# MLP and second norm of a streaming encoder step: four engines in program order, weight splits one tile ahead

## Chip, cores and metric

One core of a Trainium2 chip. The time is that of one execution of the program on the device, in microseconds (us), the median of several runs.

## What is computed

One layer of a hybrid streaming encoder for 512 prompt and 64 sample tokens (576 in all), width 1024, in float32 inputs and outputs: a modulated norm, a joint input projection, sparse attention beside a convolution module, an output projection, and then the part that the change concerns:

```python
x = x + g1 * (mix @ w_out)
h = rms_norm(x, norm2_g) * (1 + sc2) + sh2
x = x + g2 * (jnp.square(jax.nn.relu(h @ w_ff1)) @ w_ff2)
...
y_prompt = rms_norm(yp, final_g)
y_sample = rms_norm(ys, final_g)
```

`w_ff1` is 1024 x 4096, `w_ff2` 4096 x 1024. Prompt and sample have their own modulation (sc2, sh2, g2).

## The kernel before

Activations lie transposed, features on partitions, tokens along the free axis. The 576 tokens are taken in two halves of 288 (`JS`), and for the last MLP part as 320 and 256 (`LS`).

**Three matmuls for one.** Each weight tile (1024 x 128, eight blocks of 128 rows) is split into a rounded high part and the rest, both fp32r. ScalarE writes the high part (`whi`), GpSimd subtracts to get the low part (`wlo`). Activations are split likewise. `mm3` (lines 286 to 290) then multiplies high by high, high by low and low by high into one PSUM bank. So one weight tile and one token half take 24 matmuls, and a tile 48. `whi` and `wlo` have two buffers each, the raw tiles three.

**Before the MLP.** Up to the first half of the output projection, weight tiles come through `fetch`, `split` and `take` (lines 309 to 330): `take` starts the load of the tile two ahead, hands out a split tile, and issues the split of the next one in two halves of 512 columns.

**Second norm.** `out_half(mixT, norm2)` (lines 1081 to 1098) is the second half of the output projection, 192 matmuls in 16 groups on three rotating banks `ps_acc`. Behind each group `residual` (line 1078, VectorE) adds into `x`. Behind each feature tile `norm2` (lines 1182 to 1196) squares the tile on ScalarE, adds the squares into `s2x` on VectorE, and makes `h`, the operand of the first layer: ScalarE the high part, VectorE the low part. The row scale (`rbc`) is made from `s2x` later, by `spread` (lines 987 to 1004), while the first matmuls of the MLP run.

**MLP.** The 4096 hidden features are taken in four parts of eight tiles. For each part the first layer (`ff1`, lines 1218 to 1249) makes eight activation tiles `a`, and the second layer (`ff2`, `ff2_front`, lines 1251 to 1265) multiplies them with eight tiles of `w_ff2` into `x`. Where the second layer follows the first (called a join here), `ff2_front` runs the blocks of the first seven activation tiles for the first weight tiles, and then those of the eighth. To evacuate a half of `ff1`, VectorE multiplies by the row scale into `z`, ScalarE applies Relu with the bias, VectorE squares, ScalarE writes the high part of `a`, VectorE the low part (lines 1242 to 1248).

**What sets the order.** Through the output projection and the MLP the order of TensorE is the program's only within `out_half`. Everything else in the MLP, on all engines, is ordered by the scheduler. Weight tiles are loaded and split by `load_w` and `split_w` (lines 156 to 168), in whole tiles. The first tile of each part and layer, and all eight of the last second layer, get buffers of their own, named `wl`:

```python
def own_w():
    return [ft_([128, NK, 128], FR, "wl") for _ in range(2)]
...
hi, lo, _ = split_w("f1", *(own_w() if m == 0 else ()))
```

**The end.** The last part runs all eight tiles on the first 320 tokens, then transposes and finishes three row tiles (`final`, `finish`, lines 1293 to 1314), then runs the other 256 tokens with the last two row tiles between and behind.

## Time and profile before

| what | value |
|---|---|
| median of 3 runs | 887.25 us (885.54 to 888.99) |
| profiled execution | 887.81 us, of which 885.8 us span (first to last instruction) |
| mean granted TensorE clock | 0.963 |
| busy, share of the span | TensorE 92%, VectorE 58%, ScalarE 45%, GpSimd 33% |

The profile is of one execution. Engines: PE is TensorE's matmuls, PEld its weight loads, DVE VectorE, ACT ScalarE, POOL GpSimd, SP the engine that issues the loads. A name as L113 is a line of the kernel; a helper's line stands for all that call it, so L104 is every copy of ScalarE. Times in the trace count from the start of the span. [...] A row of idle time names what the engine waited for last.

### The profile page before, as it was taken

Reading aid. Unit: us, or ns where it says so; the run is one execution under the profiler, and the core shown is the slowest. Engines: PE = TensorE matmul, PEld = TensorE weight load, DVE = VectorE, ACT = ScalarE, POOL = GpSimd, SP = SyncE. Lnnn points to the kernel's source line nnn. Section 1 sums busy time; section 2 is a strip of 40 time slices with the busy share of each in tenths; the row PEclk is TensorE's granted clock in tenths of the full one; section 3 lists DMA queues with packets and bytes.
Section 4 is the critical chain, followed back from the end, with each engine's and each line's share of the span. In section 5 each row is a group of like instructions: output and inputs, shape, how many; then the busy total and the mean of one; then the engine's idle time right before and its main releaser. Section 6 shows DMA issues by size and latency. Waiting matters only on the chain. (4 is left out here: it accounts for less than half of the span.)

```text
span 885.8 us, 17048 instructions
## 1 busy us (share of the span) xinstructions
PE 815.4 (92%) x6787; PEld 758.7 (86%) x6787; DVE 509.6 (58%) x1133; ACT 402.0 (45%) x897; POOL 294.9 (33%) x273
## 2 busy tenths in 40 slices
PE   4898997977988999999899899998999989999996
PEld 3697894657877888989899899997999989999995
DVE  3579879999996344645856412663126631266343
ACT  5365554555876787554454211442124421244322
POOL 1155423122435323232423243332433333333700
PEclk9799998989999999999999899998999989999999
DMA  8984165445434356542312223222232223222411
GB/s 233 302 219 122 36 179 131 118 97 145 114 94 120 100 153 177 161 120 72 90 41 85 72 72 90 79 72 72 72 96 73 72 72 87 81 72 72 143 61 47
DMA packets 164553, 95.55 MB, mean 108 GB/s; under 512 B 7699, under 2 KB 161119, under 8 KB 164475
## 3 DMA queue, kind: packets, MB, share of 16 engines
q1 hardware_dynamic: 164475, 94.48, 38.3%
q8 instruction: 53, 0.87, 0.4%
q14 instruction: 25, 0.20, 0.1%
HBM read 88.82 MB, written 5.64 MB: 107 GB/s over the span
## 5 line engine op out<-in xcount | busy, mean ns | idle before, releaser
L113 POOL TENSOR_TENSOR wlo<-wraw,whi 128x1024 fp32r<-128x1024 f32 x52 | 125.0, 2403 | 239.0 <-ACT whi L104 230.0
L288 PE MATMUL ps_acc<-h,whi 128*128 128x288 f32 (+1 forms) x608 | 190.2, 313 | 0.0
L289 PE MATMUL ps_acc<-h,whi 128*128 128x288 f32 (+1 forms) x608 | 181.2, 298 | 0.0
L290 PE MATMUL ps_acc<-h,wlo 128*128 128x288 f32 (+1 forms) x608 | 180.8, 297 | 0.0
L104 ACT ACTIVATE whi<-wraw 128x512 fp32r<-128x512 f32 (+1 forms) x112 | 90.6, 823 | 151.4 <-PE ps_acc L289 49.0
L323 POOL TENSOR_TENSOR wlo<-wraw,whi 128x512 fp32r<-128x512 f32 x60 | 80.0, 1349 | 159.3 <-ACT whi L104 159.0
L288 PEld LDWEIGHTS ps_acc<-h,whi 128*128 128x128 f32 x608 | 115.9, 191 | 14.0 <-issue 12.7
L289 PEld LDWEIGHTS ps_acc<-h,whi 128*128 128x128 f32 x608 | 116.1, 191 | 0.9
L290 PEld LDWEIGHTS ps_acc<-h,wlo 128*128 128x128 f32 x608 | 116.0, 191 | 0.0
L1246 DVE TENSOR_TENSOR z<-z 128x288 f32<-128x288 f32 x64 | 79.3, 1242 | 43.4 <-ACT z L1245 43.4
L1078 DVE SCALAR_TENSOR_TENSOR x<-ps_acc,mod,x 128x288 f32<-128x288 f32 (+4 forms) x90 | 35.8, 422 | 95.5 <-PE ps_acc L290 95.3
L104 ACT ACTIVATE a<-z 128x288 fp32r<-128x288 f32 x64 | 28.2, 443 | 79.4 <-DVE z L1246 79.4
L555 DVE SCALAR_TENSOR_TENSOR yc<-u,cw,yc 128x606 f32<-128x606 f32 x60 | 58.6, 984 | 0.6
L1245 ACT ACTIVATE z<-z,bs 128x64 f32<-128x64 f32 (+2 forms) x96 | 39.9, 449 | 34.4 <-DVE z L1242 34.3
L113 DVE TENSOR_TENSOR a<-z,a 128x288 fp32r<-128x288 f32 x64 | 35.4, 556 | 29.7 <-ACT a L104 28.7
L738 ACT ACTIVATE gc<-sful,sg 128x544 bf16<-128x544 f32 x48 | 35.8, 746 | 32.1 <-DVE sg L736 31.3
L288 PE MATMUL ps_acc<-a,whi 128*128 128x288 f32 x168 | 49.9, 297 | 0.0
L290 PE MATMUL ps_acc<-a,wlo 128*128 128x288 f32 x168 | 49.9, 297 | 0.0
L289 PE MATMUL ps_acc<-a,whi 128*128 128x288 f32 x168 | 49.8, 297 | 0.0
L289 PE MATMUL ps_lg<-h,whi 128*128 128x290 f32 (+1 forms) x160 | 47.4, 296 | 0.0
L290 PE MATMUL ps_lg<-h,wlo 128*128 128x290 f32 (+1 forms) x160 | 47.3, 296 | 0.0
L288 PE MATMUL ps_lg<-h,whi 128*128 128x290 f32 (+1 forms) x160 | 47.2, 295 | 0.0
(359 smaller groups left out, 2110.1 us busy)
## 6 DMA issues: line engine op xcount, KB each, us to landing
wraw<-w_ff SPq DMA_DIRECT2D x64, 512.0 KB
ada<-w_ada SPq DMA_DIRECT2D x44, 512.0 KB
wraw<-w_in SPq DMA_DIRECT2D x24, 512.0 KB
wraw<-w_out SPq DMA_DIRECT2D x8, 512.0 KB
rep<-ud SPq DMA_DIRECT2D x24, 115.0 KB
xtok<-x_prompt SPq DMA_DIRECT2D x4, 512.0 KB
ada<-w_ada SPq DMA_DIRECT2D x8, 256.0 KB
ct<-cache_k SPq DMA_DIRECT2D x8, 256.0 KB
```

What stands on the lines that cost most here:

```text
L104: act.activation(out, in_, AF.Copy, scale=1.0 if scale is None else scale)
L113: eng.tensor_tensor(out, a, b, op=OP.subtract)
L288: pe.matmul(out, lhsT=hi, rhs=src[:, 0, cs_], start=first, stop=False)
L289: pe.matmul(out, lhsT=hi, rhs=src[:, 1, cs_], start=False, stop=False)
L290: pe.matmul(out, lhsT=lo, rhs=src[:, 0, cs_], start=False, stop=last)
L323: behind[0] = pool.tensor_tensor(lo[:, c], raw[:, c], f(hi[:, c]), op=OP.subtract).ins
L555: dve.scalar_tensor_tensor(yc[c], src, w, yc[c], op0=OP.mult, op1=OP.add)
L738: act.activation(eq, sful, AF.Sign, bias=cands[:, z:z + 1], scale=-1.0, accum_out=cnts[:, z:z + 1])
L1078: dve.scalar_tensor_tensor(xm[:, a:b], t[:, a - r.start:b - r.start], mod[:, g, s, m:m + 1], xm[:, a:b], op0=OP.mult, op1=OP.add)
L1245: act.activation(q, q, AF.Relu, bias=bs[:, s:s + 1])
L1246: dve.tensor_tensor(z[:, 1, r], z[:, 0, r], z[:, 0, r], op=OP.mult)
```

## The change

Four edits, all between the second half of the output projection and the end. First, TensorE, ScalarE, VectorE and GpSimd follow the program's order there (`manual_schedule`); before, only TensorE did, and in `out_half` alone. Second, the MLP's weight tiles join the one line of `fetch`, `split` and `take`, so each is split in two halves while the tile before it is multiplied; only the last eight get buffers of their own (`stay`). The front-first order at a join now covers one tile (two at the last join) instead of two (four). Third, in the evacuation ScalarE squares, into the PSUM bank that the matmuls have left, and VectorE copies and subtracts from there; these two are put off (`owed`, `settle`) until behind VectorE's next product. Fourth, `norm2` runs by token halves, its squares go to PSUM, and its VectorE work is put off likewise. At the end, the three first row tiles are finished between the last groups, and the last two together.

```diff
+    for part in range(NP_):
+        order += [f_rows(w_ff1, 0, 128 * (KP * part + m)) for m in range(KP)]
+        order += [f_rows(w_ff2, 128 * KP * part, 128 * m) for m in range(NK)]
+    stay = []
...
-            hi = wgt.tile([128, 1024], FR, name="whi", tag="whi", bufs=2)
-            lo = wgt.tile([128, 1024], FR, name="wlo", tag="wlo", bufs=2)
+            hi, lo = stay.pop(0)() if len(stay) > len(raws) + len(order) else [
+                wgt.tile([128, 1024], FR, name=nm, tag=nm, bufs=2) for nm in ("whi", "wlo")]
...
-                done(m)
+                    done(m, j)
...
+    mlp = ExitStack()
+    mlp.enter_context(tc.manual_schedule(engines={mybir.EngineType.PE, mybir.EngineType.Activation, mybir.EngineType.DVE,
+                                                  mybir.EngineType.Pool}))
     act.activation(ssq[:, 7:8], eps, AF.Sqrt)
...
-            act.activation(s2[:, 1], xm, AF.Square)
-            dve.tensor_tensor(s2[:, 0], s2[:, 0], s2[:, 1], op=OP.add)
...
+    s2 = ft_([128, TOK], FT, "s2x")
+    h2 = [ft_([128, 2, TOK + 2], FR, "h2") for _ in range(NK)]
+    for m, h in enumerate(h2):
         copy_to(act, h[:, 0, TOK:], mod[:, SH2, :, m])
+    for m, h in enumerate(h2):
         sub(dve, h[:, 1, TOK:], mod[:, SH2, :, m], f(h[:, 0, TOK:]))
...
-    with tc.manual_schedule(engines={mybir.EngineType.PE}):
-        out_half(mixT, norm2)
+    owed = []
+    def settle():
+        while owed:
+            owed.pop(0)()
+    def norm2(m, j):
+        xm, h, r = x1[m // 2][:, m % 2], h2[m], JS[j]
+        settle()
+        q = p_tp()[:, :HALF]
+        segs = [(slice(HALF * j + o, HALF * j + e), mod[:, SC2, s, m:m + 1]) for o, e, s in SEGS[j]]
+        for c, a in segs:
+            act.activation(h[:, 0, c], xm[:, c], AF.Copy, scale=a)
+        act.activation(q, xm[:, r], AF.Square)
+        def rest():
+            for c, a in segs:
+                dve.scalar_tensor_tensor(h[:, 1, c], xm[:, c], a, f(h[:, 0, c]), op0=OP.mult, op1=OP.subtract)
+            if m == 0:
+                copy_to(dve, s2[:, r], q)
+            else:
+                dve.tensor_tensor(s2[:, r], q, s2[:, r], op=OP.add)
+        owed.append(rest)
+    out_half(mixT, norm2)
+    settle()
...
+    def weight():
+        return [w.rearrange("p (k c) -> p k c", k=NK) for w in take()]
+    def group(t, w, src, r, ks):
+        for k in ks:
+            mm3(t, (w[0][:, k], w[1][:, k]), src[k], r, k == 0, k == NK - 1)
+    FRONT, LAST = range(NK - 1), range(NK - 1, NK)
+    JX = (slice(0, HALF), slice(HALF, TOK + 2))
+    def ff1(ts, parts=(range(NK),)):
+        w = weight()
+        for ks in parts:
             for j in (1, 0):
...
+                if j not in ts:
+                    ts[j] = p_ff()[:, :HALF + 2 * j]
+                group(ts[j], w, h2, JX[j], ks)
             yield
...
+    def ff1_evac(ts):
         a = ft_([128, 2, TOK], FR, "a")
-        z = big.tile([128, 2, TOK], FT, name="z", tag="b")
+        z = mt([128, TOK], FT, "z")
         bs = sml.tile([128, 2], FT, name="bs", tag="bs")
         copy_to(dve, bs, ts[1][:, HALF:HALF + 2])
...
-            dve.tensor_tensor(z[:, 0, r], ts[j][:, :HALF], rbc[:, r], op=OP.mult)
+        def half(j):
+            r, q = JS[j], ts[j][:, :HALF]
+            dve.tensor_tensor(z[:, r], q, rbc[:, r], op=OP.mult)
+            settle()
             for o, e, s in SEGS[j]:
-                q = z[:, 0, HALF * j + o:HALF * j + e]
-                act.activation(q, q, AF.Relu, bias=bs[:, s:s + 1])
-            dve.tensor_tensor(z[:, 1, r], z[:, 0, r], z[:, 0, r], op=OP.mult)
-            copy_to(act, a[:, 0, r], z[:, 1, r])
-            sub(dve, a[:, 1, r], z[:, 1, r], f(a[:, 0, r]))
...
+                y = z[:, HALF * j + o:HALF * j + e]
+                act.activation(y, y, AF.Relu, bias=bs[:, s:s + 1])
+            act.activation(q, z[:, r], AF.Square)
+            def rest():
+                copy_to(dve, a[:, 0, r], q)
+                sub(dve, a[:, 1, r], q, f(a[:, 0, r]))
+            owed.append(rest)
+        half(1)
+        half(0)
+        return a
+    def first_layer(part):
+        a_ = []
+        if part == 0:
+            t0, t1 = {}, {}
+            g = ff1(t0, (FRONT, LAST))
+            scales = spread(s2, 1.0 / D, rbc, dg)
+            next(g)
+            pump(scales, 1)
+            pump(g, 2)
+            pump(ff1(t1), 2)
+            pump(scales, 2)
+            a_ += [ff1_evac(t0), ff1_evac(t1)]
+        while len(a_) < KP:
+            t = {}
+            pump(ff1(t), 2)
+            a_.append(ff1_evac(t))
+        settle()
+        return a_
+    def second_layer(ws, ms, a_, rs):
+        gs = [(m, r, p_ff()[:, :r.stop - r.start]) for m in ms for r in rs]
+        for m, r, t in gs:
+            group(t, ws[m], a_, r, FRONT)
+        for m, r, t in gs:
+            group(t, ws[m], a_, r, LAST)
             residual(t, r, m, G2)
...
     for part in range(NP_ - 1):
...
+        a_ = first_layer(part)
+        for m in range(NK):
+            ws = {m: weight()}
+            if m == 0:
+                second_layer(ws, (m,), a_, JS[::-1])
+            else:
+                for r in JS:
+                    t = p_ff()[:, :HALF]
+                    group(t, ws[m], a_, r, range(NK))
+                    residual(t, r, m, G2)
+    def kept(m):
+        if m < 4:
+            return [big.tile([128, 1024], FR, name="wl", tag="b") for _ in range(2)]
+        return [ft_([128, 1024], FR, "wl") for _ in range(2)]
+    stay += [lambda m=m: kept(m) for m in range(NK)]
+    a_ = first_layer(NP_ - 1)
...
+    def finish(i0, i1, ys):
+        n = LT[i0][1]
+        v = fs[:n, i0:i1]
+        dve.tensor_reduce(v[:, :, 4:5], v[:, :, :4], axis=AX.X, op=OP.add)
+        act.activation(v[:, :, 5:6], v[:, :, 4:5], AF.Sqrt, bias=eps[:n], scale=1.0 / D)
+        dve.reciprocal(v[:, :, 6:7], v[:, :, 5:6])
...
+    ws = [weight(), weight()]
+    second_layer(ws, (0, 1), a_, LS[:1])
+    for m in range(2, NK):
+        ws.append(weight())
+        t = p_ff()[:, :320]
+        group(t, ws[m], a_, LS[0], range(NK))
+        residual(t, LS[0], m, G2)
     ys = [big.tile([128, D], FT, name="y", tag="b") for _ in range(2)]
     for m in range(NK):
...
+        t = p_ff()[:, :TOK - 320]
+        group(t, ws[m], a_, LS[1], range(NK))
+        residual(t, LS[1], m, G2)
+        if m < 3:
+            o, n = LT[m]
+            y = ft_([128, D], FT, "y")
+            final(m, o, n, (0, 1, 2, 3), y, p_lg)
+            final(m, o, n, (4, 5, 6, 7), y, p_tp)
+            finish(m, m + 1, (y,))
         for ks in ((0, 1, 2, 3), (4, 5, 6), (7,)):
             if ks[-1] == m:
                 for i, p in ((3, p_lg), (4, p_tp)):
                     final(i, *LT[i], ks, ys[i - 3], p)
...
+    finish(3, 5, ys)
```

The order rows below name tiles as the trace does: `whi`, `wlo`, `wl` are weight parts, `wraw` a raw tile, `z` and `a` as above, `h_...` the first layer's operand, `ps_...` PSUM banks; a trailing number such as 128x288 is the size, x2 a repetition.

ScalarE at the first join, where the last tiles of the first layer (part 0) are evacuated. Before:

```order
L104 ACTIVATE whi<-wraw 128x1024
L1245 ACTIVATE z<-z,bs 128x288
L104 ACTIVATE a<-z 128x288
L1245 ACTIVATE z<-z,bs 128x224
L1245 ACTIVATE z<-z,bs 128x64
L104 ACTIVATE a<-z 128x288
L104 ACTIVATE wl<-wraw 128x1024
L104 ACTIVATE whi<-wraw 128x1024
L1245 ACTIVATE z<-z,bs 128x288
L104 ACTIVATE a<-z 128x288
L104 ACTIVATE whi<-wraw 128x1024 x7
```

The first second-layer tile (`wl`) and the second (`whi`) were split between the two halves of the last evacuation. Now, the last two evacuations and what stands between and behind them:

```order
L1266 ACTIVATE z<-z,bs 128x224
L1266 ACTIVATE z<-z,bs 128x64
L1267 ACTIVATE ps_lg<-z 128x288
L1266 ACTIVATE z<-z,bs 128x288
L1267 ACTIVATE ps_lg<-z 128x288
L106 ACTIVATE whi<-wraw 128x512 x2
L1266 ACTIVATE z<-z,bs 128x224
L1266 ACTIVATE z<-z,bs 128x64
L1267 ACTIVATE ps_acc<-z 128x288
L1266 ACTIVATE z<-z,bs 128x288
L1267 ACTIVATE ps_acc<-z 128x288
L106 ACTIVATE whi<-wraw 128x512 x18
```

An evacuation is the five rows from `L1266 ... 128x224` to its second Square. The split of the join's first tile is the row `whi x2` between the last two evacuations; the second tile's is the first two of the eighteen halves behind the last one.

ScalarE behind the second norm, from the row scale to the split of the fourth tile (tile 3). Before:

```order
L104 ACTIVATE rbc<-ps_tp 128x512
L104 ACTIVATE rbc<-ps_tp 128x64
L1245 ACTIVATE z<-z,bs 128x288
L1245 ACTIVATE z<-z,bs 128x224
L1245 ACTIVATE z<-z,bs 128x64
L1245 ACTIVATE z<-z,bs 128x224
L104 ACTIVATE a<-z 128x288
L1245 ACTIVATE z<-z,bs 128x64
L1245 ACTIVATE z<-z,bs 128x288
L104 ACTIVATE a<-z 128x288 x3
L104 ACTIVATE whi<-wraw 128x1024
```

The scheduler mixed the first two tiles' evacuations. Now:

```order
L106 ACTIVATE rbc<-ps_tp 128x64
L1266 ACTIVATE z<-z,bs 128x224
L1266 ACTIVATE z<-z,bs 128x64
L1267 ACTIVATE ps_lg<-z 128x288
L1266 ACTIVATE z<-z,bs 128x288
L1267 ACTIVATE ps_lg<-z 128x288
L1266 ACTIVATE z<-z,bs 128x224
L1266 ACTIVATE z<-z,bs 128x64
L1267 ACTIVATE ps_acc<-z 128x288
L1266 ACTIVATE z<-z,bs 128x288
L1267 ACTIVATE ps_acc<-z 128x288
L106 ACTIVATE whi<-wraw 128x512 x2
```

The evacuations of tiles 0 and 1 stand one behind the other, and the split of tile 3 (last row) behind both.

VectorE in the first layer, one tile's evacuation in the steady stretch. Before:

```order
L108 COPY bs<-ps_lg 128x2
L1242 TENSOR_TENSOR z<-ps_lg,rbc 128x288
L1246 TENSOR_TENSOR z<-z 128x288
L113 TENSOR_TENSOR a<-z,a 128x288
L1242 TENSOR_TENSOR z<-ps_lg,rbc 128x288
L1246 TENSOR_TENSOR z<-z 128x288
L113 TENSOR_TENSOR a<-z,a 128x288
```

Product, square and subtraction of a half stood together. Now:

```order
L110 COPY bs<-ps_lg 128x2
L1262 TENSOR_TENSOR z<-ps_lg,rbc 128x288
L110 CAST a<-ps_av 128x288
L115 TENSOR_TENSOR a<-ps_av,a 128x288
L1262 TENSOR_TENSOR z<-ps_lg,rbc 128x288
L110 CAST a<-ps_lg 128x288
L115 TENSOR_TENSOR a<-ps_lg,a 128x288
```

The square is gone, and between a product and its own cast and subtraction stands the next half's product.

## Rows read from the trace of the kernel before

**Rows 1.** The page's busy totals: us, share of the span, instructions.

```profile
PE 815.4 (92%) x6787; PEld 758.7 (86%) x6787; DVE 509.6 (58%) x1133; ACT 402.0 (45%) x897; POOL 294.9 (33%) x273
```

**Rows 2.** Stretches: length, busy us of each engine, granted clock, DMA share, GB/s.

```profile
457.34:489.42 32.08, 32.08 (x243) 32.08 (x241) 23.35 (x40) 16.67 (x36) 11.99 (x5) 1.00 0.24 67
508.84:547.13 38.29, 38.29 (x290) 38.29 (x289) 7.37 (x20) 6.37 (x6) 14.34 (x6) 1.00 0.28 79
834.82:848.93 14.11, 14.11 (x98) 14.11 (x97) 2.46 (x5) 1.06 (x1) 3.88 (x2) 1.00 0.00 1
432.37:448.43 16.06, 13.41 (x96) 12.97 (x97) 8.69 (x12) 4.80 (x9) 4.98 (x2) 1.00 0.28 77
489.42:508.84 19.42, 15.64 (x98) 15.05 (x97) 6.56 (x12) 4.09 (x8) 4.92 (x2) 0.82 0.29 82
598.49:618.31 19.82, 15.50 (x98) 14.93 (x97) 6.77 (x13) 4.37 (x8) 4.91 (x2) 0.83 0.28 80
707.80:727.51 19.71, 15.40 (x98) 14.82 (x97) 6.76 (x12) 4.37 (x8) 4.91 (x2) 0.83 0.28 81
817.06:834.82 17.76, 15.89 (x98) 15.62 (x97) 7.57 (x8) 8.01 (x11) 15.50 (x7) 0.90 0.62 178
406.16:432.37 26.21, 25.97 (x194) 25.50 (x193) 22.41 (x50) 13.29 (x32) 9.54 (x7) 1.00 0.27 75
```

**Rows 3.** Waits from 430 us on, TensorE's: total us, times, longest.

```profile
PE ps_acc L288 <- ACT wl L104: 7.3, 2, 3.9
PE ps_lg L288 <- ACT wl L104: 5.0, 2, 3.9
PE ps_acc L290 <- POOL wl L113: 2.7, 3, 1.9
PE ps_lg L290 <- POOL wl L113: 1.9, 2, 1.5
```

**Rows 4.** Timeline at the first join, ScalarE and GpSimd: start, duration, idle before.

```profile
490.54 0.72 ACT L1245 ACTIVATE z<-z,bs 128x224 f32<-128x224 f32 x2 [0.96 <-DVE z L1242]
492.13 1.04 ACT L104 ACTIVATE wl<-wraw 128x1024 fp32r<-128x1024 f32 x1
493.25 2.37 POOL L113 TENSOR_TENSOR wl<-wraw,wl 128x1024 fp32r<-128x1024 f32 x1 [4.47 <-ACT wl L104]
```

**Rows 5.** Groups by shape from 400 us on: busy us, mean ns, idle before.

```profile
L1246 DVE TENSOR_TENSOR z<-z 128x288 f32<-128x288 f32 x64 | 79.3, 1242 | 43.4 <-ACT z L1245 43.4
L104 ACT ACTIVATE a<-z 128x288 fp32r<-128x288 f32 x64 | 28.2, 443 | 79.4 <-DVE z L1246 79.4
L1245 ACT ACTIVATE z<-z,bs 128x288 f32<-128x288 f32 x32 | 17.1, 533 | 2.9 <-DVE z L1242 2.9
L1242 DVE TENSOR_TENSOR z<-ps_acc,rbc 128x288 f32<-128x288 f32 x32 | 14.3, 448 | 0.5 <-PE ps_acc L290 0.5
L323 POOL TENSOR_TENSOR wlo<-wraw,whi 128x512 fp32r<-128x512 f32 x6 | 8.1, 1371 | 15.6 <-ACT whi L104 15.6
L1188 DVE TENSOR_TENSOR s2x<-s2x 128x576 f32<-128x576 f32 x7 | 7.6, 1082 | 1.0 <-ACT s2x L1187 1.0
L104 ACT ACTIVATE whi<-wraw 128x512 fp32r<-128x512 f32 x6 | 3.5, 622 | 0.9 <-ACT h L104 0.7 <-PE ps_acc L289 0.2
L1299 DVE TENSOR_TENSOR y<-ps_lg,fg 128x512 f32<-128x512 f32 x3 | 2.1, 684 | 0.2 <-PE ps_lg L1297 0.2
```

**Rows 6.** Timeline of TensorE: matmuls ahead of which it stood still.

```profile
437.40 0.40 PE L288 MATMUL ps_lg<-h,wl 128*128 128x290 f32 x1 [1.14 <-ACT wl L104]
440.08 0.53 PE L290 MATMUL ps_lg<-h,wl 128*128 128x290 f32 x2 [1.49 <-POOL wl L113]
819.39 0.42 PE L290 MATMUL ps_acc<-a,wl 128*128 128x320 f32 x1 [1.87 <-POOL wl L113]
877.26 0.30 PE L1297 MATMUL ps_lg<-ident,x 128*128 128x128 f32 x1 [0.60 <-DVE x L1078]
```

More of the change, by code (lines that the diff above doesn't have):

```diff
@@ L31 @@
 FF = 4096
+NP_ = 4
+KP = FF // 128 // NP_
 W = 31
@@ L1231, in ff1 @@
+    def group(t, w, src, r, ks):
[6 more added lines that the diff above has]
+        for ks in parts:
+            for j in (1, 0):
+                if j not in ts:
+                    ts[j] = p_ff()[:, :HALF + 2 * j]
+                group(ts[j], w, h2, JX[j], ks)
             yield
-            part((NK - 1,))
-        else:
-            part(range(NK))
@@ L1243, in ff1 @@
             for o, e, s in SEGS[j]:
-                q = z[:, 0, HALF * j + o:HALF * j + e]
-                act.activation(q, q, AF.Relu, bias=bs[:, s:s + 1])
-            dve.tensor_tensor(z[:, 1, r], z[:, 0, r], z[:, 0, r], op=OP.mult)
-            copy_to(act, a[:, 0, r], z[:, 1, r])
-            sub(dve, a[:, 1, r], z[:, 1, r], f(a[:, 0, r]))
-        yield a
-    def ff2(w, a_, m, r, t=None, ks=range(KP)):
-        if t is None:
-            t = p_ff()[:, :r.stop - r.start]
-        for k in ks:
-            mm3(t, (w[0][:, k], w[1][:, k]), a_[k], r, k == 0, k == KP - 1)
-        if ks[-1] == KP - 1:
-            residual(t, r, m, G2)
-        return t
@@ L1285, in step_kernel @@
-    a_ = [list(ff1(FF // 128 - KP + m))[-1] for m in range(KP)]
+                y = z[:, HALF * j + o:HALF * j + e]
[26 more added lines that the diff above has]
+        return a_
@@ L1301, in final @@
         act.activation(junk[:n, :w], t[:n, :w], AF.Square, accum_out=fs[:n, i, ks[0] // 2:ks[0] // 2 + 1])
-    def finish(i, o, n, y):
-        v = fs[:n, i]
-        dve.tensor_reduce(v[:, 4:5], v[:, :4], axis=AX.X, op=OP.add)
-        act.activation(v[:, 5:6], v[:, 4:5], AF.Sqrt, bias=eps[:n], scale=1.0 / D)
-        dve.reciprocal(v[:, 6:7], v[:, 5:6])
-        dve.tensor_scalar(y[:n, :512], y[:n, :512], v[:, 6:7], None, op0=OP.mult)
-        act.activation(y[:n, 512:], y[:n, 512:], AF.Copy, scale=v[:, 6:7])
-        for c in (slice(0, 512), slice(512, D)):
-            if o < SEQ:
-                nc.sync.dma_start(io["y_prompt"][0, o:min(o + n, SEQ), c], y[:min(n, SEQ - o), c])
-            if o + n > SEQ:
-                nc.sync.dma_start(io["y_sample"][0, :, c], y[SEQ - o:n, c])
@@ L1316, in step_kernel @@
-    pool.memset(fs, 0.0)
-    ws = []
-    for m in range(NK):
-        load_w("f2", w_ff2, FF - 128 * KP, 128 * m)
-        if m < 4:
-            hl = [big.tile([128, NK, 128], FR, name="wl", tag="b") for _ in range(2)]
-        else:
-            hl = own_w()
-        ws.append(split_w("f2", *hl))
-        if m == 3:
-            ff2_front(ws, a_, LS[:1])
-        elif m > 3:
-            ff2(ws[m], a_, m, LS[0])
-    for i, (o, n) in enumerate(LT[:3]):
-        y = ft_([128, D], FT, "y")
-        final(i, o, n, (0, 1, 2, 3), y, p_lg)
-        final(i, o, n, (4, 5, 6, 7), y, p_tp)
-        finish(i, o, n, y)
+    def finish(i0, i1, ys):
[4 more added lines that the diff above has]
+        dve.reciprocal(v[:, :, 6:7], v[:, :, 5:6])
+        for i, y in zip(range(i0, i1), ys):
+            o = LT[i][0]
+            dve.tensor_scalar(y[:n, :512], y[:n, :512], fs[:n, i, 6:7], None, op0=OP.mult)
+            act.activation(y[:n, 512:], y[:n, 512:], AF.Copy, scale=fs[:n, i, 6:7])
+            for c in (slice(0, 512), slice(512, D)):
+                if o < SEQ:
+                    nc.sync.dma_start(io["y_prompt"][0, o:min(o + n, SEQ), c], y[:min(n, SEQ - o), c])
+                if o + n > SEQ:
+                    nc.sync.dma_start(io["y_sample"][0, :, c], y[SEQ - o:n, c])
@@ L1340, in step_kernel @@
                     final(i, *LT[i], ks, ys[i - 3], p)
-    for i in (3, 4):
-        finish(i, *LT[i], ys[i - 3])
+    finish(3, 5, ys)
+    mlp.close()
 _INS = ["x_prompt", "x_sample", "c_prompt", "c_sample", "cache_k", "cache_v", "cache_kidx", "state_conv", "w_ada",
```

58 lines of the change are left out of this document (3 added, 55 removed).

## Prediction, made before the changed kernel was run

> **What bounds the kernel now.** I read the busy totals first: TensorE is busy for 92% of the span, so only two things can move the end, the time in which TensorE stands still and the time in which its matmuls run slow [rows 1]. Then I read the MLP stage by stretches [rows 2]. A weight tile is 48 matmuls of 288 columns. Where nothing is waited for, five tiles of the first layer take 32.08 us, 6.42 each, and six of the second 38.29, 6.38 each, at a granted clock of 1.00. A last-part tile on 320 tokens is 24 matmuls, and four of them take 14.11. Against these I lay the five stretches in which the MLP begins, or a first layer meets its second. Each holds the matmuls of two tiles (the last: of four short ones):
>
> - start: 16.06 − 2 × 6.42 = 3.2 us too long
> - first three joins: 19.42, 19.82 and 19.71 − 2 × 6.38 = 6.7, 7.1 and 6.9
> - last join: 17.76 − 14.11 = 3.7
>
> Together 27.5 us (27.6 by the rounded terms). The view of TensorE's waits names the cause: nearly all of its waiting in the MLP is on "wl", the privately buffered tile that opens each stretch, 7.3 + 5.0 us for ScalarE's high part and 2.7 + 1.9 for GpSimd's low part, 16.9 in all [rows 3]. The other 10.6 us are no waits. [...] The timeline of the first join shows why wl is late [rows 4]: ScalarE takes it up only at 492.13, behind the Relus of the evacuation, though the join began at 489.42, and GpSimd starts at 493.25 and needs 2.37 us more.
>
> **The change, part by part.** (a) The weight split. In the new order ScalarE splits tile m+1 between the evacuations of m−1 and m, everywhere, and the joins lose their special buffers (the last part alone keeps its tiles). Is the tile ready? Take T as the end of group m−1. VectorE starts some 0.2 later, then 0.45 for the product, 0.53 Relu, and a Square [rows 5]. No row has ScalarE writing PSUM. The nearest is its 0.443 for the same 288 columns from SBUF to SBUF; I take 0.45, with 0.35 and 0.60 as ends. So the split starts at about T+1.65, its high halves (0.62 each) end by T+2.9, and GpSimd's halves (1.37 each) by T+3.7 and T+5.0 [rows 5]. TensorE asks for the first low half at T+6.7 and for the second 1.6 later. The slack is 3.0 us or more in every steady group, so this hides under matmuls.
>
> At the three inner joins the second tile is split after the last evacuation, on ScalarE from T+1.65, ready by T+5.0, wanted at T+6.4. The last activation tile is ready at about T+2.7, and TensorE has 42 matmuls over the first seven tiles, 5.6 us, before it asks. Nothing is late there: 20.7 us come back, waits and slow clock together. At the last join the second tile is wanted after 21 short matmuls, T+3.1, its low half at T+3.4, against T+3.7: I charge 0.3 (0 to 1.0). The gain there is 3.4.
>
> (b) The start. Both first tiles are split during the output projection or just behind it, so the two waits of 1.14 and 1.49 [rows 6] go: 3.2 back. The sum of squares must be there when the seven-tile front of the first group ends, 5.6 us behind the projection. VectorE then holds a residual, three products and an add, and ScalarE three copies and a Square, about 5 us with GpSimd in between. I charge 0.3 (0 to 1.5).
>
> (c) A new wait. After the row scale is ready (call it R), two tiles are evacuated back to back, and ScalarE must run both before the split of tile 3, as the order rows of ScalarE show. Each half goes from VectorE to ScalarE and back, in a fixed turn. By 0.45 per product, 0.45 per cast or subtraction (taken as the product's row), 0.72 for a Relu pair [rows 4], 0.53 for a single Relu and 0.45 per Square, ScalarE finishes at R+5.3; its first high half is there at R+5.9 and GpSimd's first low half at R+7.2. TensorE has begun tile 2 about 0.9 before R and wants tile 3's low half at R+5.9. I charge 1.3 (0 to 2.5). Later groups recover, by the slack above.
>
> (d) VectorE one group late. The z-square leaves VectorE; it cost 1.242 on average where a product that reads PSUM costs 0.448 [rows 5]. It is squared by ScalarE into PSUM instead, and VectorE's copy and subtraction now read PSUM. VectorE's time is worth nothing by itself in these groups, as TensorE never waits for it there [rows 3]; I count 0. What hides it is 6.4 us of matmuls per tile; without that cover it would be the chain of (c).
>
> [...]
>
> (e) Second norm by halves. VectorE was busy 22.41 of the 26.21 us of the projection that feeds it [rows 2]. The adds go from 1.08 [rows 5] to two of 0.45 per tile, 1.3 us less in all; one product piece more per tile adds at most 8 × 0.45 = 3.6, taken as a whole product's row, so at most 24.7. That still fits under 26.2: 0 (from −0.5, what 26.21 stands above 192 matmuls at 6.42 per 48, to +3).
>
> (f) The end. Three row tiles are finished between the last groups instead of before them. Their chain on VectorE (residual, two products of 0.68 [rows 5], reduction, reciprocal, product) is about as long as a group plus its transposes, since it waits for ScalarE's two passes over the same tile. So the fourth residual comes late and the transposes behind it wait, as they did for 0.60 at 877.26 [rows 6]. With the joint finish of the last two tiles I charge 1.2 (−0.5 to +3).
>
> **Sum.** 27.5 − 0.3 − 0.3 − 1.3 − 1.2 = 24.4 us. The profiled execution took 887.81 (span 885.8 and 2.0 around it), which gives 863.4. The median of the runs, 887.25, lies 0.6 lower, so I forecast **863 us**.
>
> **The rivals.**
> 1. *The new short waits cost the clock.* Against it, the two idles of 1.14 and 1.49 at the start left the clock at 1.00; for it, one of 1.87 at the last join [rows 6] came with 0.90 and cost 3.7 − 1.9 = 1.8 beyond the idle [rows 2]. Three such places, (c), the last join and (f), give 863 + 5 = 868. [...]
> 2. *VectorE's fixed order holds up the projection.* The residual that frees a bank now stands behind the late half of the tile before. GpSimd runs 9.54 us there [rows 2] and can block each product. If half of that falls on VectorE, 24.7 + 4.8 = 29.5, and TensorE, which took 26.2, loses 3 to 5 us there and at the start: 866 to 868.
> 3. *The joins keep part of their wait*, because a low half comes 1 us late and the clock falls each time: 4 × (1 + 1.8) = 11, 874.
> 4. *Slower: ScalarE becomes the weight supplier that is late in every first-layer group.* It decides once the chain of (a) is more than 3.0 us longer than I worked out. At 4.0 longer each of 29 groups waits 1.0, 863 + 29 = 892. Against it: ScalarE was busy 16.67 of 32.08 us [rows 2].
> 5. *Nothing happens.* Only if the engines did not follow the written order; the order rows show that they do.
>
> **How the numbers follow.** Forecast with its bounds, 859.5 to 866: 0.64. Rival 1: 0.15. Rival 2: 0.12. Rival 3: 0.05. Rival 4: 0.02. Rival 5 and unnamed: 0.02. The best case, with no new cost, is 887.25 − 27.5 = 859.8. From 859.5 to 868.5 the range takes in the first two cases and half of the third, a little over 8 in 10. A measurement here tells 0.5%, 4.4 us, from no change. All but rivals 4 and 5 are beyond it: faster 0.96, same 0.015, slower 0.025.
>
> **What would show it.** Right: three inner joins at 6.4 us per tile and clock 1.00, no "wl" among TensorE's waits but at the last join, the z-square at about 0.45 on ScalarE, one wait of 1 to 1.5 us before tile 3 of the first part, and a short one in the last groups. Wrong: a clock below 1.00 behind 440 us, waits on the split in many groups, or a projection longer than 27 us.

## The result, and the profile after

The changed kernel took **860.26 us** (median of 4 runs, 859.93 to 861.67), against 888.12 of the kernel before; the ratio is 0.968 (95% interval 0.966 to 0.971). The forecast was 863, in a range of 859.5 to 868.5. The profiled execution has a span of 858.6 us, 27.2 less than before. One of the four runs of joins_ahead, below, took 1220.0 us at a mean clock of 0.587, and its median there is that of the other three.

The page's busy totals, which answer to [rows 1]: TensorE is busy for 94% of a shorter span, VectorE has 61 us less to do.

```profile
PE 808.2 (94%) x6787; PEld 753.0 (88%) x6787; DVE 449.0 (52%) x1148; ACT 412.5 (48%) x976; POOL 303.5 (35%) x337
```

The stretches of the changed kernel from the second half of the output projection to the end, columns as in [rows 2]: projection, first layer, then second and first layers in turn, then the last part's 320 tokens, its 256 tokens, and what lies behind the last matmul.

```profile
404.98:430.54 25.56, 25.56 (x194) 25.56 (x194) 24.00 (x67) 17.82 (x53) 10.89 (x8) 1.00 0.23 64
430.54:485.80 55.26, 54.37 (x403) 53.38 (x402) 22.73 (x63) 28.11 (x63) 20.39 (x16) 1.00 0.27 78
485.80:536.74 50.94, 50.94 (x386) 50.94 (x385) 10.75 (x27) 10.11 (x18) 20.30 (x16) 1.00 0.32 91
536.74:588.10 51.36, 51.36 (x387) 51.36 (x386) 19.55 (x53) 24.41 (x54) 20.44 (x16) 1.00 0.27 76
588.10:638.93 50.83, 50.83 (x386) 50.83 (x385) 10.75 (x27) 10.09 (x18) 20.36 (x16) 1.00 0.32 91
...
690.29:741.27 50.98, 50.98 (x386) 50.98 (x385) 10.75 (x27) 10.10 (x18) 20.23 (x16) 1.00 0.32 90
...
792.61:821.11 28.50, 28.37 (x194) 28.10 (x193) 5.96 (x12) 8.72 (x16) 17.57 (x14) 1.00 0.36 109
821.11:850.23 29.12, 28.04 (x234) 27.07 (x232) 13.60 (x37) 9.24 (x26) 0.00 (x0) 1.00 0.14 46
850.23:858.60 8.37, 0.00 (x0) 0.00 (x0) 1.61 (x6) 2.26 (x7) 0.00 (x0) 0.69 0.44 126
```

Each line holds whole groups, so the same cuts through the trace of before give the balance:

| stretch | before | after | gain | forecast |
|---|---|---|---|---|
| up to the projection's second half (not changed) | 406.16 | 404.98 | 1.2 | 0 |
| second half of the projection | 26.21 | 25.56 | 0.65 | 0 |
| first layer, part 0 (start, row scale, tile 3) | 57.05 | 55.26 | 1.8 | 3.2 − 0.3 − 1.3 = 1.6 |
| three second layers (inner joins) | 57.71, 57.98, 57.90 | 50.94, 50.83, 50.98 | 20.8 | 20.7 |
| three more first layers | 51.36, 51.33, 51.36 | 51.36, 51.36, 51.34 | 0 | 0 |
| last part, 320 tokens (last join) | 31.87 | 28.50 | 3.4 | 3.4 |
| last part, 256 tokens, and the end | 36.87 | 37.49 | −0.6 | −1.2 |

TensorE's waits from 400 us on, against [rows 3], are down to four; the clock is 1.00 in every stretch with matmuls.

```profile
PE ps_lg L1334 <- DVE x L1087: 1.1, 3, 0.6
PE ps_lg L292 <- POOL wlo L332: 0.8, 1, 0.8
```

The list puts waits with the same cause together: the first line is three waits at the end, the second is tile 3 of part 0. The timelines of ScalarE, GpSimd and TensorE (start, duration) show how the latter comes about: R, the end of the row scale, is 446.57.

```profile
445.86 0.71 ACT L106 ACTIVATE rbc<-ps_tp 128x512 f32<-128x512 f32 x2 [6.22 <-PE ps_tp L1009]
...
451.50 0.41 ACT L1267 ACTIVATE ps_acc<-z 128x288 f32<-128x288 f32 x1
451.86 1.14 ACT L106 ACTIVATE whi<-wraw 128x512 fp32r<-128x512 f32 x2
```

```profile
452.55 2.52 POOL L332 TENSOR_TENSOR wlo<-wraw,whi 128x512 fp32r<-128x512 f32 x2 [10.82 <-ACT whi L106]
```

```profile
452.15 0.29 PE L292 MATMUL ps_av<-h,wlo 128*128 128x288 f32 x1
452.52 0.41 PE L290 MATMUL ps_lg<-h,whi 128*128 128x290 f32 x1
453.88 0.40 PE L292 MATMUL ps_lg<-h,wlo 128*128 128x290 f32 x1 [0.81 <-POOL wlo L332]
```

Matmuls that wait for nothing start 0.13 us apart here. Three steps behind the last one of tile 2 (452.15) the first low half was wanted at 452.55, R + 6.0. It was used at 453.88, 1.3 us late. The list shows 0.81 of this, because the high half ahead of it came late too (452.52).

And a steady group. Its predecessor ended at T = 466.54, when TensorE took up the next one; the low half that GpSimd makes here is wanted from 473.22 on.

```profile
466.54 0.29 PE L290 MATMUL ps_acc<-h,whi 128*128 128x290 f32 x1
473.22 0.30 PE L292 MATMUL ps_lg<-h,wlo 128*128 128x290 f32 x1
```

```profile
467.80 0.41 ACT L1267 ACTIVATE ps_acc<-z 128x288 f32<-128x288 f32 x1
468.15 1.14 ACT L106 ACTIVATE whi<-wraw 128x512 fp32r<-128x512 f32 x2
```

```profile
468.84 2.56 POOL L332 TENSOR_TENSOR wlo<-wraw,whi 128x512 fp32r<-128x512 f32 x2 [3.86 <-ACT whi L106]
```

The split starts at T + 1.6, both low halves are there at T + 4.9 and wanted from T + 6.7.

### The profile page after: what moved, and what is told of

Same layout as the page of the kernel before. It is cut to its first block, busy times and chain, and to the rows that moved or that the text cites. A ratio compares the mean times of both kernels' runs of the same rounds, so it can differ in the third digit from the quotient of the medians.

```text
span 858.6 us, 17186 instructions
## 1 busy us (share of the span) xinstructions
PE 808.2 (94%) x6787; PEld 753.0 (88%) x6787; DVE 449.0 (52%) x1148; ACT 412.5 (48%) x976; POOL 303.5 (35%) x337
## 4 chain that ended last, share of the span: by engine, by line
PE 69%; DVE 17%; ACT 7%; DMA 3%; issue 3%; POOL 1%; SPq 0%; ACTq 0%; DVEq 0%; POOLq 0%
PE ps_acc L290 11%; PE ps_acc L291 11%; PE ps_acc L292 11%; PE ps_lg L292 5%; PE ps_lg L290 5%; PE ps_lg L291 5%; DVE yc L564 3%; PE ps_av L292 3%; PE ps_av L290 2%; PE ps_av L291 2%; DVE score L690 2%; DVE m L688 2%; PE ps_tp L234 2%; DMA ada<-w_ada 1%; PE ps_av L887 1%
## 5 line engine op out<-in xcount | busy, mean ns | idle before, releaser
L332 POOL TENSOR_TENSOR wlo<-wraw,whi 128x512 fp32r<-128x512 f32 x172 | 222.6, 1314 | 378.3 <-ACT whi L106 378.0
L106 ACT ACTIVATE whi<-wraw 128x512 fp32r<-128x512 f32 x172 | 99.8, 621 | 126.4 <-issue 120.6
L1266 ACT ACTIVATE z<-z,bs 128x224 f32<-128x224 f32 (+2 forms) x96 | 40.2, 450 | 98.6 <-DVE z L1262 98.6
L1087 DVE SCALAR_TENSOR_TENSOR x<-ps_acc,mod,x 128x288 f32<-128x288 f32 (+3 forms) x91 | 36.2, 420 | 83.6 <-PE ps_acc L292 83.0
L290 PE MATMUL ps_acc<-a,whi 128*128 128x288 f32 x192 | 56.6, 295 | 0.0
L291 PE MATMUL ps_acc<-a,whi 128*128 128x288 f32 x192 | 56.6, 295 | 0.0
L292 PE MATMUL ps_lg<-h,wlo 128*128 128x288 f32 (+1 forms) x176 | 52.2, 296 | 0.8 <-POOL wlo L332 0.8
L291 PE MATMUL ps_lg<-h,whi 128*128 128x288 f32 (+1 forms) x176 | 52.2, 297 | 0.0
L290 PE MATMUL ps_lg<-h,whi 128*128 128x288 f32 (+1 forms) x176 | 52.2, 296 | 0.1
L872 POOL TENSOR_SCALAR prob<-prob,mx 128x128 f32<-128x128 f32 (+3 forms) x32 | 20.2, 631 | 56.8 <-DVE mx L871 34.2
L292 PE MATMUL ps_lg<-a,wlo 128*128 128x288 f32 x128 | 37.8, 295 | 0.0
L290 PE MATMUL ps_lg<-a,whi 128*128 128x288 f32 x128 | 37.8, 295 | 0.0
```

The costliest lines, as they stand in the source:

```text
L106: act.activation(out, in_, AF.Copy, scale=1.0 if scale is None else scale)
L290: pe.matmul(out, lhsT=hi, rhs=src[:, 0, cs_], start=first, stop=False)
L291: pe.matmul(out, lhsT=hi, rhs=src[:, 1, cs_], start=False, stop=False)
L292: pe.matmul(out, lhsT=lo, rhs=src[:, 0, cs_], start=False, stop=last)
L332: behind[0] = pool.tensor_tensor(lo[:, c], raw[:, c], f(hi[:, c]), op=OP.subtract).ins
L872: pool.tensor_scalar(pt[:, :n], pt[:, :n], m[:, 1:2], 1.0, op0=OP.mult, op1=OP.mult)
```

## The experiments

Up to the second half of the projection TensorE executes the same instructions in the same order in all kernels, and yet that half began between 403.90 and 407.21 us. Differences of a microsecond are therefore read from the stretches, and totals are compared as **the rest**: from the start of that half to the end of the span, in the one profiled execution of each kernel.

| kernel | ratio to before (95%) | median us | the rest, us | against the change |
|---|---|---|---|---|
| before | 1 | 888.1 | 479.64 | +26.0 |
| the change | 0.968 (0.966 to 0.971) | 860.3 | 453.62 | |
| before_ahead | 0.975 (0.973 to 0.978) | 868.1 | 461.43 | +7.8 |
| joins_ahead | 0.974 (0.970 to 0.979) | 865.4 | 459.61 | +6.0 |
| order_off | 0.970 (0.967 to 0.974) | 863.3 | 456.07 | +2.5 |
| join_late | 0.973 (0.969 to 0.977) | 865.5 | 458.90 | +5.3 |
| zsq_dve | 0.968 (0.964 to 0.971) | 860.7 | 453.20 | −0.4 |
| split_whole | 0.973 (0.969 to 0.977) | 865.3 | 458.05 | +4.4 |
| norm_whole | 0.970 (0.967 to 0.974) | 862.4 | 454.53 | +0.9 |
| front_off | 0.968 (0.966 to 0.970) | 861.5 | 453.59 | 0 |
| end_old | 0.972 (0.970 to 0.975) | 865.6 | 457.09 | +3.5 |
| tile3_early | 0.966 (0.961 to 0.970) | 858.7 | 452.22 | −1.4 |
| best | 0.966 (0.964 to 0.968) | 858.9 | 451.93 | −1.7 |

### One thing alone in the kernel before: the split at the inner joins (before_ahead)

```diff
-        a_ = [list(g)[-1] for g in todo]
-        ws = []
-        for m in range(2):
-            load_w("f2", w_ff2, 128 * KP * part, 128 * m)
-            ws.append(split_w("f2", *(own_w() if m == 0 else ())))
+        a_ = [list(g)[-1] for g in todo[:-1]]
+        pump(todo[-1], 1)
+        load_w("f2", w_ff2, 128 * KP * part, 0)
+        ws = [split_w("f2", *own_w())]
+        a_ += [list(todo[-1])[-1]]
+        load_w("f2", w_ff2, 128 * KP * part, 128)
+        ws.append(split_w("f2"))
```

> The kernel before, with one thing alone: at the three inner joins the load and the split of the second layer's first tile are written ahead of the evacuation of the last first-layer group instead of behind it; the scheduler, the whole tiles, the squares on VectorE, the private buffer, the old norm and end all stay. In ScalarE's order three instructions move, one per join, by seven rows. Theory: this is what emptied the inner joins, so about 20 of the 27 us come with it: 866 to 869 us, and each join's waits on wl go. Rival A (the written order of four engines or the relief of VectorE is needed too, since the evacuation's long squares beside GpSimd make the next tile late): the joins keep half, 875 to 880. Rival B (the private tile was late for its transfer or its buffer, not for its place): no change, 887.

Its stretches, first layer of part 0 and the three second layers:

```profile
432.31:490.87 58.56, 55.95 (x400) 54.97 (x401) 35.02 (x60) 27.30 (x55) 20.02 (x9) 0.97 0.23 66
490.87:541.88 51.01, 51.01 (x387) 51.01 (x386) 14.81 (x30) 9.68 (x13) 18.68 (x8) 1.00 0.32 91
...
593.22:644.61 51.39, 51.20 (x386) 50.97 (x385) 15.09 (x31) 9.86 (x13) 19.23 (x8) 1.00 0.31 90
...
695.96:747.41 51.45, 51.27 (x386) 51.04 (x385) 15.10 (x31) 9.85 (x13) 19.30 (x8) 1.00 0.31 90
```

The three second layers fell from 57.71, 57.98 and 57.90 to 51.01, 51.39 and 51.45: **19.7 us from three moved splits**, with the scheduler, whole tiles, long squares and private buffers all still there. Rivals A and B fall. In the kernel before the tile was late for its place in the program, behind an evacuation whose results its split did not need. The start grew by 1.5 with the same waits and a lower clock (below).

### The last join too (joins_ahead)

```diff
-    a_ = [list(ff1(FF // 128 - KP + m))[-1] for m in range(KP)]
+    a_ = [list(ff1(FF // 128 - KP + m))[-1] for m in range(KP - 1)]
+    g = ff1(FF // 128 - 1)
+    pump(g, 1)
+    ws = [last_w(0)]
+    a_ += [list(g)[-1]]
```

> The run before_ahead with the same move at the last join too: the load and split of the first of the last eight tiles are written ahead of the evacuation of the last first-layer group. Theory: the first tile's wait of 1.9 us goes, but the second tile, wanted 3.1 us after the join began, is still split behind the evacuation in one piece and is 1 to 2 us late, so that the last join keeps part of its 3.7: 866.5 us, against 868.1 of before_ahead. Rival (place of the first tile is all): the whole 3.4 come back, 864.7. Rival (GpSimd, busy for 15.5 of 17.8 us there, sets the pace): no gain, 868.

The last part's 320 tokens took 28.8 us (800.56 to 829.37) instead of 31.9; of the first tile's wait of 1.87 nothing is left, and the second waits 0.41. The rival that the first tile's place is all comes nearest: 3.1 of the 3.4 came back.

```profile
800.56:829.37 28.81, 28.40 (x194) 28.13 (x193) 11.01 (x15) 9.58 (x13) 17.14 (x7) 1.00 0.32 96
```

The rest fell by only 1.8 because the start, which has not changed, took 1.2 more in this profile than in before_ahead's; the clock granted there is not shown. So four moved splits carry 22.8 of the 26.0 us.

### The engines' order given back to the scheduler (order_off)

```diff
-    mlp.enter_context(tc.manual_schedule(engines={mybir.EngineType.PE, mybir.EngineType.Activation, mybir.EngineType.DVE,
-                                                  mybir.EngineType.Pool}))
+    mlp.enter_context(tc.manual_schedule(engines={mybir.EngineType.PE}))
```

> The changed kernel with ScalarE, VectorE and GpSimd given back to the scheduler (TensorE alone follows the program's order); the halves, the one line of weights, the squares in PSUM and the second norm by halves stay. The scheduler then puts each split between the two halves of an evacuation, half a group (3.2 us) later than the written order. Theory: that eats the whole slack of 3.0 us, so the first low half comes 0.1 to 0.3 us late in some 30 groups: 863 to 869 us at a clock of 1.00. Rival: the buffers and the halves do all of it and the order nothing, 860 us. [...]

The total lies in the expected band, but not for that reason. The expectation took the evacuation between whose halves the split stands for that of the running group; it is that of the group before. So the scheduler splits about 1.5 us earlier than the written order, not later (at 466.39, 0.1 behind the end of a group, instead of 1.6), and no steady group waits. Part 0's first layer even took 53.84 instead of 55.26, with no wait before tile 3. All of the loss, 4.3 us, lies in the last first layer (55.60 against 51.34), in one wait:

```profile
788.82 0.40 PE L292 MATMUL ps_acc<-h,wlo 128*128 128x290 f32 x1 [2.25 <-POOL wlo L332]
```

The timelines of ScalarE and GpSimd there show the scheduler's order: splits of the last eight tiles (`wl`) stand ahead of that of the tile wanted next (`whi`, `wlo`), and the first of them has waited for its transfer.

```profile
781.35 0.63 ACT L106 ACTIVATE wl<-wraw 128x512 fp32r<-128x512 f32 x1 [4.18 <-DMA wraw<-w_ff]
...
785.36 1.14 ACT L106 ACTIVATE whi<-wraw 128x512 fp32r<-128x512 f32 x2
```

```profile
785.01 2.52 POOL L332 TENSOR_TENSOR wl<-wraw,wl 128x512 fp32r<-128x512 f32 x2 [0.40 <-ACT wl L106]
787.50 2.51 POOL L332 TENSOR_TENSOR wlo<-wraw,whi 128x512 fp32r<-128x512 f32 x2
```

The written order of ScalarE, VectorE and GpSimd is worth 2.5 us in all: 4.3 at this place, less 1.4 at tile 3 and 0.4 in the last part.

### The split put late at two joins (join_late)

```diff
         half(1)
+        if mid:
+            mid()
         half(0)
+        if end:
+            end()
```

`mid` and `end` are `split` for the last evacuation of part 0 and of part 1; the split ahead is left out there.

> The changed kernel, but at two of the three inner joins the split of the second layer's first tile is put later: at the first join between the two halves of the last evacuation (about 1.6 us before the last first-layer group ends), at the second join behind the whole evacuation (about 1.6 us after it); the third join stays as it is. Theory of the prediction: the split ahead is what emptied the joins. First join: the first low half comes 0.2 to 0.4 us after it is wanted, at a clock of 1.00, +0.3 us. [...] Third: 0. Together about 867 us. [...] Rival (waiting and clock are separate, and a single join keeps the clock): 864 us.

First join: one wait of 0.29, stretch 51.51 against 50.94, +0.6, clock 1.00. Second join, TensorE's timeline:

```profile
589.85 0.40 PE L290 MATMUL ps_lg<-a,whi 128*128 128x288 f32 x1 [2.11 <-ACT whi L106]
591.21 0.61 PE L292 MATMUL ps_lg<-a,wlo 128*128 128x288 f32 x1 [0.83 <-POOL wlo L332]
```

and by stretches behind it (granted clock third from the end):

```profile
589.85:592.00 2.15, 1.32 (x5) 1.09 (x6) 0.38 (x1) 1.50 (x3) 2.13 (x2) 0.69 0.00 0
592.00:594.00 2.00, 2.00 (x10) 2.00 (x9) 0.00 (x0) 0.00 (x0) 2.00 (x3) 0.50 0.11 33
594.00:596.00 2.00, 2.00 (x16) 2.00 (x16) 0.00 (x0) 0.00 (x0) 0.87 (x1) 0.98 0.77 230
```

The two stretches that meet there grew by 2.3 and 2.5, 4.8 in all, 2.9 of it listed waits and 1.8 more, most of it at the lower clock. The theory's places are right. Of its 867, 860.3 for the change and 0.3 for the first join leave 6.4 for the second, and no run shows that much: 4.8 came. The rival fails, since the clock fell to 0.50 (592 to 594 us).

### The square back on VectorE (zsq_dve)

```diff
-            act.activation(q, z[:, r], AF.Square)
...
-                copy_to(dve, a[:, 0, r], q)
-                sub(dve, a[:, 1, r], q, f(a[:, 0, r]))
+                dve.tensor_tensor(z[:, 1, r], z[:, 0, r], z[:, 0, r], op=OP.mult)
+                copy_to(dve, a[:, 0, r], z[:, 1, r])
+                sub(dve, a[:, 1, r], z[:, 1, r], f(a[:, 0, r]))
```

> The changed kernel with the square of z back on VectorE, from SBUF to SBUF, and the high part copied by ScalarE, still one half later. Theory: VectorE's time is covered by 6.4 us of matmuls per tile, so the steady groups lose nothing although the square stretches beside GpSimd to about 1.2 us; only where two evacuations stand back to back (before tile 3 of the first part) is the chain longer, by 1 to 4 us: 861 to 865 us. [...]

The copy stayed on VectorE, contrary to what the expectation says, so VectorE carries still more and ScalarE less. The time did not grow (−0.4 by the rest), and tile 3 waits the same 0.81, where ScalarE's two evacuations have two Squares less each: there ScalarE waits for VectorE's products instead (1.37 and 0.85 us). VectorE's relief is worth nothing here. The square, by groups, and for comparison VectorE's and GpSimd's timelines in the kernel before:

```profile
L1269 DVE TENSOR_TENSOR z<-z 128x288 f32<-128x288 f32 x64 | 39.7, 620 | 0.4 <-ACT z L1266 0.4
```

```profile
562.10 2.28 DVE L1246 TENSOR_TENSOR z<-z 128x288 f32<-128x288 f32 x1 [0.61 <-ACT z L1245]
566.57 0.46 DVE L1246 TENSOR_TENSOR z<-z 128x288 f32<-128x288 f32 x1 [0.79 <-ACT z L1245]
```

```profile
561.66 2.40 POOL L113 TENSOR_TENSOR wlo<-wraw,whi 128x1024 fp32r<-128x1024 f32 x1 [4.48 <-ACT whi L104]
```

In the kernel before, the long square started inside GpSimd's piece of 2.40 us, took 2.28 us instead of 0.46 and ended 0.3 behind the piece. In zsq_dve half of the squares take 0.45 and the longest 1.309, about as long as GpSimd's half pieces (1.305 on average).

### Halves or whole tiles (split_whole)

```diff
-            for c in (slice(0, 512), slice(512, 1024)):
+            for c in ((slice(0, 1024),) if len(order) < 61 else (slice(0, 512), slice(512, 1024))):
```

> The changed kernel with the MLP's weight tiles split in one piece of 1024 columns on ScalarE and GpSimd instead of two of 512 (from the first layer's third tile on). Theory: the halves pay only where a tile is split late. Steady groups and the inner joins keep their slack (ready about 5.1 us after the group before ended, wanted at 6.4): no wait. Tile 3 of the first part gets its low half about 1.4 us later, and the second tile of the last join about 1.4 later: +2.8 us at a clock of 1.00, 863. [...] Rival (halves matter in every group, as ScalarE is held longer): above 870.

```profile
453.11 0.40 PE L290 MATMUL ps_lg<-h,whi 128*128 128x290 f32 x1 [0.50 <-ACT whi L106]
455.55 0.61 PE L292 MATMUL ps_lg<-h,wlo 128*128 128x290 f32 x1 [1.91 <-POOL wlo L332]
800.91 0.41 PE L292 MATMUL ps_av<-a,wl 128*128 128x320 f32 x1 [1.61 <-POOL wl L332]
```

TensorE's new waits are at the two places named and nowhere else. Tile 3's stretch grew by 3.0 (58.24 against 55.26), with a clock of 0.50 behind the wait:

```profile
455.55:458.00 2.45, 2.45 (x10) 2.45 (x11) 0.00 (x0) 0.44 (x1) 1.93 (x1) 0.50 0.41 116
```

The last part's 67.44 us from its join to the end are 1.5 more than the change's 65.99; there the matmuls behind the wait of 1.61 came 0.15 us apart, the pace of the last-part tiles at a clock of 1.00 [rows 2]. The result, 865.3, lies 2.3 above the theory's 863 and below the rival's 870, then: one of the two places lost clock.

### Parts that might cost nothing (front_off, norm_whole, end_old)

```diff
-            if m == 0:
-                second_layer(ws, (m,), a_, JS[::-1])
-            else:
-                for r in JS:
+            if True:
+                for r in (JS[::-1] if m == 0 else JS):
```

> The changed kernel without the front-first order at the three inner joins: the second layer's first tile takes one half after the other, each over all eight activation tiles. Theory: nothing is lost, since half 1 of the last activation tile is wanted 2.8 us after the join began and comes at about 1.6, and half 0 is wanted at 6.0 and comes at 2.7: 860.3 us, as the changed kernel. [...]

No wait, 453.59 against 453.62: with half 1 taken first, the front-first order at the inner joins does nothing.

For norm_whole, the old norm under the written order:

```diff
-        act.activation(q, xm[:, r], AF.Square)
...
-                dve.tensor_tensor(s2[:, r], q, s2[:, r], op=OP.add)
+            act.activation(sq, xm, AF.Square)
+            dve.tensor_tensor(s2, s2, sq, op=OP.add)
```

> The changed kernel with the second norm by whole feature tiles again, as in the kernel before (squares in SBUF, one addition of 576 columns by VectorE per tile, nothing put off), but under the written order. Theory: VectorE's work of 23 to 25 us still fits beside the projection's 25.6, which stays within 26.2, and the sum of squares comes at most 1 us later: 860.3 to 861.5 us. Rival 2 of the prediction (a fixed order on VectorE holds up the residuals that free PSUM banks, as an operation on two SBUF inputs can be held by GpSimd): the projection takes 28 us or more and the start more too, 863 to 866.

The projection took 26.54 instead of 25.56, with one listed wait of 0.44 for a residual; behind it nothing differs (427.99 against 428.06). VectorE's and GpSimd's timelines ahead of that wait:

```profile
421.62 0.76 DVE L1214 TENSOR_TENSOR s2x<-s2x,z 128x576 f32<-128x576 f32 x1 [0.81 <-ACT z L1213]
425.03 1.23 DVE L1214 TENSOR_TENSOR s2x<-s2x,z 128x576 f32<-128x576 f32 x1 [0.81 <-ACT z L1213]
```

```profile
423.04 2.60 POOL L332 TENSOR_TENSOR wlo<-wraw,whi 128x512 fp32r<-128x512 f32 x2 [4.68 <-ACT whi L106]
```

The add ahead of the late residual took 1.23 us where it started beside GpSimd, and 0.76 where GpSimd was idle. The norm's products did the same in the kernel before: 1.42 us beside GpSimd and 0.75 without. A residual, which reads PSUM, took 0.50 beside GpSimd, as it did without (424.83 us).

```profile
421.57 0.50 DVE L1078 SCALAR_TENSOR_TENSOR x<-ps_acc,mod,x 128x288 f32<-128x288 f32 x1
422.00 1.42 DVE L1193 SCALAR_TENSOR_TENSOR h<-x,mod,h 128x512 fp32r<-128x512 f32 x1
425.44 0.75 DVE L1193 SCALAR_TENSOR_TENSOR h<-x,mod,h 128x512 fp32r<-128x512 f32 x1
```

```profile
420.33 2.54 POOL L323 TENSOR_TENSOR wlo<-wraw,whi 128x512 fp32r<-128x512 f32 x2 [3.80 <-ACT whi L104]
```

The theory's direction holds, 0.3 beyond its bound of 26.2. Rival 2's delay is there, at under half of its price: 1.0 in the projection, where it said 2.4 or more, and nothing at the start. VectorE's load is not the reason, since it was busy for 19.57 us there and for 24.00 in the change.

For end_old, the three first row tiles go back to one place and the last two are finished apart:

```diff
+    for m, (o, n) in enumerate(LT[:3]):
+        ...
+        finish(m, m + 1, (y,))
...
-    finish(3, 5, ys)
+    finish(3, 4, ys[:1])
+    finish(4, 5, ys[1:])
```

> The changed kernel with the end as in the kernel before: the three first row tiles are transposed and finished between the two halves of the last layer, and the last two are finished apart. The prediction charged 1.2 us for the new end; the stretches of the two traces show 0.7. Theory: the old end is 0.5 to 1 us shorter, 859.5 us. Rival: under the written order the three row tiles in a row make TensorE wait for PSUM banks that VectorE and ScalarE empty, 1 us or more longer, 861.5.

```profile
829.16 0.38 PE L290 MATMUL ps_lg<-a,wl 128*128 128x256 f32 x1 [2.41 <-ACT junk L1338]
```

The rival is right, and more so than it said: under the written order TensorE's next group stands behind all three row tiles and waits 2.41 us for a bank that ScalarE still reads. The clock behind it stayed at 1.00:

```profile
829.16:831.16 2.00, 2.00 (x17) 2.00 (x18) 1.03 (x4) 1.55 (x4) 0.00 (x0) 1.00 0.43 159
```

Under the written order the old end is 3.5 us longer.

### Better than both (tile3_early, best)

```diff
-            a_ += [ff1_evac(t0), ff1_evac(t1)]
+            a_.append(ff1_evac(t0))
+            split()
+            hold.append(1)
+            a_.append(ff1_evac(t1))
```

> The changed kernel with the split of tile 3 of the first part between the two evacuations behind the row scale, instead of behind both. Theory: its wait (0.8 listed, 1.1 by the stretch) goes, and nothing else becomes late, since the second evacuation is wanted 6 us later: 859.2 us, first-part stretch about 1.1 shorter. Rival: the second evacuation, put off by 1.2 us of splitting, holds PSUM banks or the next splits back, and the wait only moves: 860.3.

(`hold` makes the next `take` leave out its own split.) The stretch is 53.84 instead of 55.26, without any wait: 1.4 us, more than the listed wait of 0.81 and close to the 1.3 by which the low half came late.

```profile
429.74:483.58 53.84, 53.84 (x402) 53.33 (x401) 22.71 (x63) 28.11 (x63) 20.41 (x16) 1.00 0.28 80
```

For `best` the second halves of the last row tile's output are issued by ScalarE's queue:

```diff
+                q = nc.scalar if i == 4 and c.start else nc.sync
```

> The changed kernel with the split of tile 3 between the two evacuations (as in the run tile3_early, 858.7) and, at the end, the last three output transfers of the last row tile issued by ScalarE's queue instead of SyncE's, where six stand in a row at about 0.6 us each. Theory: the end behind the last matmul shrinks from 8.5 to about 7.5 us, 857.8. Rival: the transfers' landing sets the end, not their issue, 858.7.

Two transfers go by ScalarE's queue (the expectation says three), and the six issues of the change took 0.34 to 0.60 us each (it says about 0.6). The last issue ended 4.8 us behind the start of the last matmul instead of 5.8, but the span's end came only 0.3 nearer. The last packet of the transfers ended 6.9 us behind that matmul instead of 7.2: the rival is right, the landing sets the end. tile3_early and best are the fastest kernels here. By their times they can be told neither from each other nor from the change (their intervals overlap); the 1.4 us is read from the stretch.

## Why the prediction was right

**(a) The split ahead** carried the forecast: 20.8 us at the inner joins against 20.7, 3.4 at the last against 3.4, where the charge of 0.3 answers to 28.50 us against 2 × 14.11. The chain was worked out to a tenth: split at T + 1.6 (T + 1.65), second low half at T + 4.9 (T + 5.0), the Square into PSUM 0.415 us (0.45, from bounds of 0.35 and 0.60). What it did not see is how little of the change does this: before_ahead and joins_ahead get it in the old program.

**(b) The start.** The two waits on `wl` are gone, and the charge of 0.3 fell away: the front of the first group ran without a wait. With the split of tile 3 moved too, the stretch is 53.84 (tile3_early), 3.2 below the 57.05 of before, which is the 3.2 that was counted. No run makes the early split of the first two tiles alone, so this term is read from the trace and not tested.

**(c) Tile 3.** ScalarE finished the two evacuations 5.34 us behind R (5.3 forecast); the first low half was used at R + 7.3 (7.2) and wanted at R + 6.0 (5.9). It was late by the 1.3 charged, and by tile3_early the place costs 1.4. The list shows a wait of 0.81, below the 1 to 1.5 that the prediction named as its sign.

**(d) VectorE one group late** counted 0. zsq_dve confirms that the relief of VectorE is worth nothing; it keeps the lateness, which no run takes away, and in the change no steady group waits.

**(e) The norm by halves** counted 0 and gave 0.65, just beyond the stated bound of 0.5. norm_whole shows that under the written order the new norm (halves, squares in PSUM and work put off, together) is worth 1.0 in the projection. The charge counted VectorE's load, forecast at most 24.7 and measured 24.00; norm_whole has less load (19.57) and is longer, with one residual late. Why the scheduler's projection took the 0.65 is not shown.

**(f) The end** was the charge most off in size: charged 1.2, measured 0.6. The fourth residual does come late, but only by 0.18 us, and two later ones by 0.29 and 0.60, of which the kernel before had the 0.60 [rows 6].

The sum of terms (a) to (f) came out 1.6 us too small (26.0 against 24.4); the other 1.2 of the span lie in the part that has not changed, and are chance, here against the forecast. The time lies only 0.8 above the lower end of the range: no charge was too small by more than 0.1, and the largest error is the 0.65 of (e) that was counted as nothing.

**Rival 1** was weighed with evidence that did not bear the weight. The prediction held against it that two idles of 1.14 and 1.49 at the start left the clock at 1.00 [rows 2, 6]. In before_ahead the same place has the same idles, and the clock fell:

```profile
437.31 0.40 PE L288 MATMUL ps_lg<-h,wl 128*128 128x290 f32 x1 [1.12 <-ACT wl L104]
440.01 0.53 PE L290 MATMUL ps_lg<-h,wl 128*128 128x290 f32 x2 [1.49 <-POOL wl L113]
```

```profile
440.00:443.00 3.00, 2.99 (x14) 2.99 (x15) 0.76 (x2) 0.00 (x0) 0.00 (x0) 0.59 0.63 178
443.00:446.00 3.00, 3.00 (x21) 3.00 (x20) 0.00 (x0) 0.00 (x0) 0.00 (x0) 0.84 0.07 20
```

The rival failed all the same: behind the change's waits (0.8, and 0.2 to 0.6 at the end) the clock stayed at 1.00. They are shorter than any single wait that cost clock in these runs, but the length alone does not decide, since 2.41 in end_old cost none; what does is open. Rival 2 did not occur in the change, whose projection has no listed wait, nor did rivals 3 to 5.

## What to carry to other kernels

Where a stretch opens with a wait on a tile that nothing held up, look for the instructions that stand ahead of its producer: moving four of them in the old program gave 22.8 of 26.0 us. Price such a wait with the half-clock stretch that can follow it (1.4 to 2.0 us beyond the wait here), and do not take a clock that held in one profile for a rule. Read how late a matmul started, since the list of waits can show less (0.81 of 1.3 at tile 3). Here, halving a producer's pieces, or writing an engine's order by hand, paid where a tile was split late and nowhere else in the MLP, and with a written order the end of the program had to be interleaved too, or it waited for its own banks.
